# Two-layer transformer trunk: MLP in two phases through DRAM, with seven block products for the latents' first product

## The chip, the cores and the metric

The kernel runs on one core of one Trainium2 chip. The metric is the device time of one execution in microseconds (us); lower is better. A core has TensorE (PE, matrix products), VectorE (DVE), ScalarE (ACT), GpSimd (POOL) and SyncE (SP), which here only issues DMAs. Each engine works through its own instructions in the order in which they stand; semaphores make one wait for another. PE reads its operands from SBUF and writes to PSUM banks, from which DVE and ACT read.

## The reference, cut to what matters

Two layers over 1024 latent tokens and 256 context tokens with 1024 features. Layer 0 mixes tokens by latent attention, layer 1 by neighbourhood attention; each is followed by a squared-ReLU MLP. Layer 1 needs the MLP of the latents alone.

```
def _mlp(h, w1, w2):
    return jnp.square(jax.nn.relu(h @ w1)) @ w2          # w1 1024 x 4096, w2 4096 x 1024

for i in range(2):
    ...
    x = _layer_norm(alpha * x + g1 * y, ln1_g[i], ln1_b[i])        # y: mixer
    x = _layer_norm(alpha * x + g2 * _mlp(x * (1 + sc2) + sh2, mlp_w1[i], mlp_w2[i]), ln2_g[i], ln2_b[i])
    # the context tokens likewise, in layer 0 only
```

## The kernel before, in words

**Arithmetic.** Every large product is made in f32 accuracy from three matmuls in a reduced format: an operand is cut into hi (a cast) and lo (the rest), and `mm3` (L63 to L67) issues hi·hi, hi·lo and lo·hi into one PSUM bank. `split_sb` (L57) makes hi by an ACT cast (L59) and lo by a subtraction on POOL or DVE (L61).

**Tokens and chunks.** Group 0 is the context (256 tokens, tiles 0 and 1), groups 1 and 2 are the latents (512 tokens each, tiles 2 to 5 and 6 to 9). The 4096 hidden features are 32 chunks of 128 (NFF), the 1024 inputs 8 slices k of 128 (KD).

**wo()** multiplies the attention's output by w_o, a token tile at a time, adds the residual, normalises (`normalise`: bn_stats on DVE, a power on POOL at L230, the last step on ACT at L549) and calls `to_hT` for each pair of tiles: PE transposes (L562), ACT applies the modulation (L566), and DVE and POOL split the result into hi and lo (`hTm`). So the MLP's input is split pair by pair.

**mlp()** goes through steps of two chunks for one group. In a step, for each chunk, the first product `pu` takes 8 slices × 3 matmuls (512 columns for a latent group, 256 for the context); ACT and DVE square the ReLU (L817, L818), ACT casts hi (`uh`) and POOL makes lo (`ul`). The second product of the step before stands behind it on PE: for each token tile two halves `py` of 2 chunks × 3 matmuls of 512 columns, added into `y` in SBUF by DVE (L778). u stays in SBUF. The last steps of each group also multiply by the gate and add the residual (`prep`, L731 and L732), normalise, and in layer 0 make the next layer's transposes (`hTa`).

**What sets the order.** The program is written in program order, and a scheduler puts each engine's instructions in an order of its own by simulated times. Tiles of a pool are reused: a new one waits until the readers of the old one are done. Weights come through three raw buffers (tag "raw", bufs=3) on SP's DMA queue, in order; stores go on ACT's queue, in order with ACT's other work.

## Time and profile before

| what | value |
|---|---|
| device time, median of 3 runs | 3207.97 us (3207.79 to 3212.2) |
| span of the profiled execution | 3209.5 us |
| PE busy | 3093.2 us, 96% of the span |
| DVE, ACT, POOL busy | 52%, 34%, 34% |
| granted TensorE clock, mean | 0.987 |
| mlp of layer 0 (first pu to last py) | about 872 to 1786 us |
| mlp of layer 1 | about 2466 to 3192.5 us |

The profiled execution is a run like the others: its span of 3209.5 us stands 1.5 us above their median. In a window row the busy time of each engine is followed by its number of instructions; what PE's busy time lacks to the window's length is PE's idle time. The granted clock is a share of 2.4 GHz; 0.5 is 1.2 GHz.

### The profile page before, as it was taken

What the parts mean: (1) busy time and instruction counts of PE and PEld (TensorE: products, weight loads), DVE (VectorE), ACT (ScalarE), POOL (GpSimd) and SP (SyncE); (2) the same over time, 40 slices, a digit from 0 to 9 for tenths busy, and PEclk for the clock granted to TensorE, in tenths of its full rate; (3) what the DMA queues carried; (4) which work ended last, traced back from release to release, by engine and by line L of the source; (5) the groups of instructions that cost most, each with busy time, mean ns of one, the idle gap of its engine ahead of it and who ended that gap; (6) DMA issues with size and microseconds to landing.
All of it is one profiled execution on the core that took longest, in us unless ns stands there. A gap on an engine that the chain in (4) does not pass through costs nothing.

```text
span 3209.5 us, 41711 instructions
## 1 busy us (share of the span) xinstructions
PE 3093.2 (96%) x16242; PEld 2590.1 (81%) x16242; DVE 1662.1 (52%) x3590; ACT 1089.9 (34%) x1899; POOL 1083.8 (34%) x772
## 2 busy tenths in 40 slices
PE   8999999999999999999998899999988999999996
PEld 4798888798878888888887788888867888888885
DVE  4345666575623333333348777777758333333358
ACT  2234444443432121111124455555543412212222
POOL 3352111112224343433227422233224344443236
PEclk8999999999999999999999999999999999999998
DMA  8445332304412111112113211111144222221122
GB/s 322 156 165 177 127 122 96 124 24 139 157 59 67 52 60 59 53 60 68 38 60 112 78 45 48 44 45 41 39 133 156 66 74 71 73 86 53 53 72 99
DMA packets 106646, 286.57 MB, mean 89 GB/s; under 512 B 9984, under 2 KB 43904, under 8 KB 100688
## 3 DMA queue, kind: packets, MB, share of 16 engines
q1 hardware_dynamic: 79536, 229.84, 21.8%
q10 hardware_dynamic: 26912, 54.05, 4.5%
q8 instruction: 128, 2.10, 0.3%
q14 instruction: 70, 0.57, 0.1%
HBM read 231.40 MB, written 52.46 MB: 88 GB/s over the span
## 4 chain that ended last, share of the span: by engine, by line
PE 85%; DVE 8%; ACT 2%; DMA 2%; issue 1%; POOL 1%; SPq 0%; ACTq 0%; DVEq 0%; POOLq 0%
PE py L65 9%; PE py L66 9%; PE py L67 9%; PE pu L65 8%; PE pu L66 8%; PE pu L67 8%; PE nj L66 3%; PE nj L65 3%; PE nj L67 3%; PE pt L487 2%; PE mps L151 2%; PE s L464 1%; PE po L66 1%; PE s L465 1%; PE s L467 1%
## 5 line engine op out<-in xcount | busy, mean ns | idle before, releaser
L778 DVE TENSOR_TENSOR y<-py,y 128x512 f32<-128x512 f32 x496 | 341.7, 691 | 533.4 <-PE py L67 533.2
L65 PE MATMUL py<-w2h,uh 128*128 128x512 f32 x1152 | 449.3, 393 | 22.3 <-DVE y L758 12.8
L66 PE MATMUL py<-w2l,uh 128*128 128x512 f32 x1152 | 448.5, 391 | 0.0
L67 PE MATMUL py<-w2h,ul 128*128 128x512 f32 x1152 | 447.3, 390 | 0.0
L61 POOL TENSOR_TENSOR ul<-r,uh 128x512 fp32r<-128x512 f32 (+1 forms) x160 | 195.0, 1219 | 419.3 <-ACT uh L59 396.6
L65 PE MATMUL pu<-hTm,whw 128*128 128x512 f32 (+1 forms) x880 | 325.9, 371 | 4.0 <-DVE r L818 3.4
L66 PE MATMUL pu<-hTm,whw 128*128 128x512 f32 (+1 forms) x880 | 325.9, 370 | 0.0
L67 PE MATMUL pu<-hTm,wlw 128*128 128x512 f32 (+1 forms) x880 | 325.5, 370 | 0.0
L818 DVE SCALAR_TENSOR_TENSOR r<-pu,r 128x512 f32<-128x512 f32 (+1 forms) x160 | 101.7, 636 | 358.7 <-ACT r L817 357.7
L65 PEld LDWEIGHTS py<-w2h,uh 128*128 128x128 f32 x1152 | 217.6, 189 | 68.2 <-DVE y L758 14.1
L67 PEld LDWEIGHTS py<-w2h,ul 128*128 128x128 f32 x1152 | 216.9, 188 | 45.9
L66 PEld LDWEIGHTS py<-w2l,uh 128*128 128x128 f32 x1152 | 217.2, 189 | 41.7
L817 ACT ACTIVATE r<-pu 128x512 f32<-128x512 f32 (+1 forms) x160 | 88.3, 552 | 447.2 <-PE pu L67 445.0
L476 POOL TENSOR_TENSOR p<-p,st 128x1280 f32<-128x1280 f32 (+1 forms) x40 | 79.2, 1979 | 381.6 <-DVE st L475 298.4
L65 PE MATMUL nj<-hTa,whn 128*128 128x512 f32 (+1 forms) x512 | 200.2, 391 | 2.2 <-ACT njt L864 2.2
L65 PEld LDWEIGHTS pu<-hTm,whw 128*128 128x128 f32 x880 | 166.9, 190 | 33.7 <-DVE r L818 3.7
L66 PEld LDWEIGHTS pu<-hTm,whw 128*128 128x128 f32 x880 | 167.0, 190 | 29.1
L67 PEld LDWEIGHTS pu<-hTm,wlw 128*128 128x128 f32 x880 | 166.9, 190 | 28.4
L67 PE MATMUL nj<-hTa,wln 128*128 128x512 f32 (+1 forms) x512 | 188.4, 368 | 0.0
L66 PE MATMUL nj<-hTa,whn 128*128 128x512 f32 (+1 forms) x512 | 187.6, 366 | 0.0
L61 POOL TENSOR_TENSOR w2l<-w2r,w2h 128x1024 fp32r<-128x1024 f32 x46 | 109.9, 2399 | 172.0 <-PE pu L67 169.6
L54 ACT CAST th<-pt 128x512 fp32r<-128x512 f32 x168 | 96.8, 585 | 162.5 <-PE pt L487 160.7
(270 smaller groups left out, 7262.6 us busy)
## 6 DMA issues: line engine op xcount, KB each, us to landing
adaw<-in_ada_w SPq DMA_DIRECT2D x40, 1024.0 KB
w2r<-in_mlp_w SPq DMA_DIRECT2D x72, 512.0 KB
raww<-in_w SPq DMA_DIRECT2D x50, 512.0 KB
rawn<-in_nqkv SPq DMA_DIRECT2D x24, 512.0 KB
w1rw<-in_w SPq DMA_DIRECT2D x22, 512.0 KB
x1d<-xr ACTq DMA_DIRECT2D x18, 512.0 KB
xa<-x1d SPq DMA_DIRECT2D x18, 512.0 KB
x1e<-xa ACTq DMA_DIRECT2D x18, 512.0 KB
```

Source lines behind the costliest of these rows:

```text
L54: nc.scalar.copy(hi, ps)
L61: return h, e.tensor_tensor(lo, src, self.f(hi), op=ALU.subtract)
L65: mm(out, lhsT=ah, rhs=bh, start=first, stop=False)
L66: mm(out, lhsT=ah, rhs=bl, start=False, stop=False)
L67: return mm(out, lhsT=al, rhs=bh, start=False, stop=last)
L151: nc.tensor.matmul(ps[32 * j:32 * j + 32, :], lhsT=self.sT[:, k, :], rhs=x, start=(k == 0), stop=(k == KD - 1), tile_position=(0, 32 * j))
L464: mm(o, lhsT=qq[:, 0, sl], rhs=kh, start=True, stop=False)
L476: (nc.vector.tensor_scalar(p[:, 0:n], p[:, 0:n], st[:, 5:6], None, op0=ALU.mult) if t % 2 else nc.gpsimd.tensor_tensor(p[:, 0:n], p[:, 0:n ...
L487: nc.tensor.transpose(pt[:, c, i, :], ps_[i][:, col:col + P], self.ident)
L778: nc.vector.tensor_tensor(y[t][:, ns], py, y[t][:, ns], op=ALU.add)
L817: nc.scalar.activation(r[:, 0:n], pu[:, 0:n], AF.Relu)
L818: nc.vector.scalar_tensor_tensor(r[:, 0:n], pu[:, 0:n], 0.0, r[:, 0:n], op0=ALU.max, op1=ALU.mult)
```

## The change

`mlp()` becomes `up()` (the first product, for all chunks) and then `down()` (the second). Between them u goes to DRAM (`ud`) as hi and lo and comes back.

In `up()`, the latents' product is taken as one of 2 × 2 blocks: the inputs' two halves of four slices k, two chunks (f0, f1 of the pair fp), and the two latent groups. Eight block products of 12 matmuls (4 slices × 3) become seven, by the Strassen-Winograd scheme. On the token side it needs A11, A12, A22 and the sums S1 to S4, each cast to hi and lo (once per layer, `split` and `comb`); on the weights' side B11, B21, B12 (with the context), B22 and T1 to T4, made for every pair of chunks (`prepare`). Products that share a summand accumulate in one PSUM bank and are read in between (`p1`, `u2`, `u3`). The context's product in layer 0 keeps its form. `wo()` no longer splits: `to_hF` leaves the modulated transposes in f32 (`hf`), and `up()` splits them.

In `down()`, blocks of 2 or 4 chunks go through all token tiles; u is loaded for each pair of tiles (`ub`, three buffers).

```diff
-    def mlp(self, l, nm, nm2):                     # two-chunk steps, u in SBUF
-            for si, (chunks, g) in enumerate(steps):
...
+    def to_hF(self, xhs, pair, hs, nm):            # called by wo() in place of to_hT
...
+                nc.scalar.activation(self.hf[g][:, k, off:off + 256], pt[:, c, :], AF.Identity,
+                                     scale=hs[:, 0, k:k + 1], bias=hs[:, 1, k:k + 1])
+    def mlp(self, l, nm, nm2, front, hpools=None):
+        self.ud = [[self.dp.tile([P, 2, n], F32, name=f"ud{l}_{f}_{g}") for g, (o, n) in enumerate(GR)]
+                   for f in range(NFF)]
+        self.up(l, nm, front)
+        self.down(l, nm, nm2, hpools)
+    def up(self, l, nm, front):
...
+            def split(n):
+                for j in range(0, 4, 2):
+                    self.split_sb(A[n][0][:, j:j + 2], A[n][1][:, j:j + 2], blk[n][:, j:j + 2], lo_eng="dve")
+            def comb(o, x, y, op):
+                for j in range(0, 4, 2):
+                    nc.vector.tensor_tensor(blk[o][:, j:j + 2], blk[x][:, j:j + 2], blk[y][:, j:j + 2], op=op)
+            split("A11")
+            split("A12")
+            if l == 0:
+                for j in range(0, 8, 4):
+                    self.split_sb(hc[0][:, j:j + 4], hc[1][:, j:j + 4], self.hf[0][:, j:j + 4], lo_eng="dve")
+            split("A22")
+            comb("S1", "A21", "A22", ALU.add)
+            comb("S3", "A11", "A21", ALU.subtract)
+            comb("S2", "S1", "A11", ALU.subtract)
+            split("S2")
+            split("S1")
+            split("S3")
+            comb("S4", "A12", "S2", ALU.subtract)
+            split("S4")
...
+                def X():
+                    h, lo = pair(self.wp, ("wh", "wl"), "x")
+                    self.split_sb(h, lo, raw[0])
+                def Ta():
+                    nc.vector.tensor_tensor(t[:, 0:4], b12, b11, op=ALU.subtract)
+                    nc.vector.tensor_tensor(t[:, 4:8], b22, t[:, 0:4], op=ALU.subtract)
+                    h, lo = pair(self.ws, ("th", "tl"), "a")
+                    self.split_sb(h, lo, t)
...
+            def put(src, f, g, n, nm_):
+                nc.scalar.copy(uhl[:, 0, 0:n], src)
+                nc.vector.tensor_tensor(uhl[:, 1, 0:n], src, self.f(uhl[:, 0, 0:n]), op=ALU.subtract)
+                nc.scalar.dma_start(self.ud[f][g], self.f(uhl[:, :, 0:n]))
+            def from_sb(ps, x, f, g, nm_):
+                nc.vector.tensor_tensor(c, ps, x, op=ALU.add)
+                nc.scalar.activation(c, c, AF.Relu)
+                nc.scalar.activation(c, c, AF.Square)
+                put(c, f, g, 512, nm_)
...
+                prod(pa, B["11"], A["A11"], True, False)
+                p1 = sb("p1")
+                nc.scalar.copy(p1, pa)
+                if fp == 0:
+                    prod(pa, B["21"], A["A12"], False, True)
+                    from_ps(pa, f0, 1, 512, f"a{l}{fp}")
+                    ctx(0, "11", "21")
+                prod(pb, B["T2"], A["S2"], True, False)
+                nc.vector.tensor_tensor(u2, pb, p1, op=ALU.add)
+                prod(pc, B["T1"], A["S1"], True, False)
+                prod(pb, B["T3"], A["S3"], False, False)
+                nc.vector.tensor_tensor(u3, pb, p1, op=ALU.add)
+                from_sb(pc, u3, f1, 2, f"d{l}{fp}")
+                if fp:
+                    prod(pa, B["21"], A["A12"], False, True)
+                    from_ps(pa, f0, 1, 512, f"a{l}{fp}")
+                    ctx(0, "11", "21")
+                prod(pb, B["T4"], A["A22"], False, True)
+                from_sb(pb, p1, f0, 2, f"c{l}{fp}")
+                prod(pc, B["22"], A["S4"], False, True)
+                from_sb(pc, u2, f1, 1, f"b{l}{fp}")
+                ctx(1, "12", "22")
+    def down(self, l, nm, nm2, hpools):
+        sizes = [2, 4, 4, 4, 4, 4, 4, 2, 4]
...
+                    wr = self.wp.tile([P, D], F32, tag="raw", bufs=3, name=f"w2r{l}{f}")
+                    nc.sync.dma_start(wr, a["mlp_w2"][l, f * P:(f + 1) * P, :])
+                    self.split_sb(h, lo, wr)
+            def load(bi, fs, p):
+                u = up.tile([P, 4, 2, 256], F32R, tag="ub", bufs=3, name=f"ub{l}{bi}{p}")
+                for i, f in enumerate(fs):
+                    nc.sync.dma_start(self.f(u[:, i]), self.ud[f][g][:, :, off:off + 256])
```

**Where instructions move, 1.** DVE at the end of wo() and the start of the MLP in layer 0. `mv0a9` is the LayerNorm of the last token tile, `hTm` the split of the last pair, `r` the first chunks' squared ReLU. Before, from the last tile on:

```order
L547 SCALAR_TENSOR_TENSOR mv0a9_9265<-mv0a9_9265 128x1
L59 CAST hTm0200_9059<-htmpm040_9278 128x256
L61 TENSOR_TENSOR hTm0201_9060<-htmpm040_9278,hTm0200_9059 128x256
L59 CAST hTm0210_9061<-htmpm041_9282 128x256
L59 CAST hTm0220_9063<-htmpm042_9291 128x256
```

In the changed kernel the same stretch of DVE holds the lo parts of `A11`, `A12`, `hc` (context) and `A22` (L61), the sums (L704, made in place in `hfm`) and the lo parts of S1 to S4:

```order
L548 SCALAR_TENSOR_TENSOR mv0a9_9124<-mv0a9_9124 128x1
L61 TENSOR_TENSOR A11l0_9263<-hfm01_8608,A11h0_9262 128x1024 x2
L61 TENSOR_TENSOR A12l0_9271<-hfm01_8608,A12h0_9270 128x1024 x2
L61 TENSOR_TENSOR hcl_9277<-hfm00_8431,hch_9276 128x1024 x2
L61 TENSOR_TENSOR A22l0_9273<-hfm02_8957,A22h0_9272 128x1024 x2
L704 TENSOR_TENSOR hfm02_8957<-hfm02_8957 128x1024 x2
L704 TENSOR_TENSOR hfm02_8957<-hfm01_8608,hfm02_8957 128x1024
L61 TENSOR_TENSOR S1l0_9267<-hfm02_8957,S1h0_9266 128x1024
L704 TENSOR_TENSOR hfm02_8957<-hfm01_8608,hfm02_8957 128x1024
L61 TENSOR_TENSOR S1l0_9267<-hfm02_8957,S1h0_9266 128x1024
L704 TENSOR_TENSOR hfm01_8608<-hfm02_8957,hfm01_8608 128x1024
L61 TENSOR_TENSOR S3l0_9269<-hfm02_8957,S3h0_9268 128x1024
```

The splits of the last pair (`hTm`, 128x256) are gone. Eight more rows of the same kind and size follow (24 operations of 128x1024 in all; 22 in layer 1, which has no `hc`), and then the first sums on the weights' side, `ta` and `tb` (128x512), from which ACT and POOL make T1 to T4. On ACT the cast of A11's hi part stands behind the eight `hf` activations of the last pair.

**Where instructions move, 2.** SP between up() and down() of layer 0, in the changed kernel. `w2r` are raw rows of w2, `ub00` the u of the first block for the three first pairs of tiles:

```order
L867 DMA w2r04_12820<-in_mlp_w2 128x1024
L867 DMA w2r05_12826<-in_mlp_w2 128x1024
L867 DMA w2r06_13033<-in_mlp_w2 128x1024
L919 DMA ub000_12773<-ud0_0_0_9163 128x512
L919 DMA ub000_12773<-ud0_1_0_9166 128x512
L919 DMA ub001_12832<-ud0_0_1_9164 128x2x256
L919 DMA ub001_12832<-ud0_1_1_9167 128x2x256
L919 DMA ub002_12867<-ud0_0_1_9164 128x2x256
L919 DMA ub002_12867<-ud0_1_1_9167 128x2x256
L867 DMA w2r07_13039<-in_mlp_w2 128x1024
```

Before, u needed no load, and SP's rows at the start of the MLP were those of the weights, the residual and the gate:

```order
L116 DMA raww1000_9353<-in_w1 128x1024
L116 DMA raww1001_9391<-in_w1 128x1024
L692 DMA w2r000_9429<-in_mlp_w2 128x1024
L692 DMA w2r001_9435<-in_mlp_w2 128x1024
L618 DMA xr08_9127<-in_xtok 128x1024
L618 DMA xr09_9200<-in_xtok 128x1024
L704 DMA w1rw1032_9665<-in_w1 128x1024
L116 DMA raww1033_9703<-in_w1 128x1024
L534 DMA ln1_g0_10041<-in_ln1_g 128x1024
```

The first loads of u stand behind the raw rows of chunks 4, 5 and 6, each of which takes over a raw buffer from chunk 1, 2 or 3. On POOL the lo parts of w2's chunks 0 to 3 stand one behind the other; ACT's cast of chunk 1 takes the buffer that the last product of up() read. Layer 1 has the same order.

**Where instructions move, 3.** ACT within up() of layer 1, around the copy of `p1` for one pair of chunks (`th`, `wh`: weights' hi parts; `cc`, `cb`: two of the four results; `ud`: a store):

```order
L59 CAST th16b_23852<-tb16_23849 128x1024
L786 ACTIVATE cc15_23841<-cc15_23841 128x512
L787 ACTIVATE cc15_23841<-cc15_23841 128x512
L773 CAST uhlc15_23845<-cc15_23841 128x512
L59 CAST wh16y_23876<-w1r113_23732 128x512
L786 ACTIVATE cb15_23868<-cb15_23868 128x512
L775 DMA ud1_10_2_22830<-uhlc15_23845 128x1024
L787 ACTIVATE cb15_23868<-cb15_23868 128x512
L813 COPY p116_23899<-sa16_23884 128x512
L773 CAST uhlb15_23872<-cb15_23868 128x512
```

The copy `p116` of the pair's first block product stands behind the work on the pair before, a store among it, which waits for DVE's lo part. On PE the product that goes on in the same bank (B21·A12) is issued three matmuls behind the end of the first product (of S1's, in another bank); in layer 0 the distance is larger, and ACT has also the context's results and one more cast (`wh`, 128x1024) ahead of the copy.

## Rows read from the trace of the kernel before

**Rows 1.** Page, parts 1 and 4: busy time by engine; the chain by engine.

```profile
PE 3093.2 (96%) x16242; PEld 2590.1 (81%) x16242; DVE 1662.1 (52%) x3590; ACT 1089.9 (34%) x1899; POOL 1083.8 (34%) x772
...
PE 85%; DVE 8%; ACT 2%; DMA 2%; issue 1%; POOL 1%; SPq 0%; ACTq 0%; DVEq 0%; POOLq 0%
```

**Rows 2.** PE in layer 0's MLP: start us, us, line, operation.

```profile
1209.80 0.39 PE L65 MATMUL pu<-hTm,whw 128*128 128x512 f32 x1
...
1212.52 0.39 PE L66 MATMUL py<-w2l,uh 128*128 128x512 f32 x1
```

**Rows 3.** Windows: length, busy us (x instructions) by engine, clock, DMA share, GB/s.

```profile
885.00:890.00 5.00, 1.32 (x8) 0.84 (x8) 4.39 (x13) 3.56 (x8) 2.39 (x4) 0.80 0.41 116
890.00:895.00 5.00, 4.88 (x12) 3.88 (x13) 3.91 (x6) 3.10 (x5) 2.38 (x3) 0.52 0.74 247
...
1690.00:1810.00 120.00, 104.08 (x478) 83.59 (x476) 105.02 (x168) 51.88 (x78) 78.40 (x64) 0.96 0.31 109
2466.00:2490.00 24.00, 17.59 (x76) 13.82 (x75) 21.77 (x47) 11.92 (x17) 10.16 (x11) 0.86 0.58 203
2550.00:2600.00 50.00, 50.00 (x222) 41.41 (x221) 15.79 (x23) 8.67 (x12) 24.11 (x13) 1.00 0.22 73
3120.00:3150.00 30.00, 27.89 (x122) 22.44 (x120) 25.57 (x17) 5.98 (x9) 23.50 (x10) 1.00 0.50 159
3150.00:3160.00 10.00, 0.34 (x1) 0.35 (x2) 8.88 (x8) 1.73 (x3) 5.28 (x3) 0.55 0.27 94
3160.00:3192.00 32.00, 30.67 (x125) 24.80 (x125) 30.42 (x58) 9.36 (x8) 18.97 (x17) 0.93 0.17 67
```

**Rows 4.** Timeline at the end of wo(), layer 0, of DVE, ACT and POOL.

```profile
872.93 1.23 DVE L649 SCALAR_TENSOR_TENSOR xr<-xr,ty 128x1024 f32<-128x1024 f32 x1
874.07 1.22 DVE L61 TENSOR_TENSOR w1lw<-w1rw,w1hw 128x1024 fp32r<-128x1024 f32 x1
875.21 1.28 DVE L543 BATCH_NORM_STATS2 bn0a<-xr 128x6 f32<-128x512 f32 x2
...
877.84 1.24 ACT L549 ACTIVATE xr<-xr,mv0a 128x1024 f32<-128x1024 f32 x1 [7.79 <-DVE mv0a L547]
...
883.95 2.01 ACT L566 ACTIVATE htmpm<-htm,hs 128x256 f32<-128x256 f32 x4 [4.87 <-PE htm L562]
```

**Rows 5.** Groups by line and shape: xcount | busy us, mean ns | idle before.

```profile
L778 DVE TENSOR_TENSOR y<-py,y 128x512 f32<-128x512 f32 x496 | 341.7, 691 | 533.4 <-PE py L67 533.2
...
L61 DVE TENSOR_TENSOR ol<-or,oh 128x1024 fp32r<-128x1024 f32 x18 | 22.2, 1235 | 12.9 <-ACT oh L59 12.9
...
L817 ACT ACTIVATE r<-pu 128x512 f32<-128x512 f32 x128 | 76.1, 594 | 294.7 <-PE pu L67 292.6 <-POOL y L762 0.4
L59 ACT CAST w2h<-w2r 128x1024 fp32r<-128x1024 f32 x72 | 73.8, 1048 | 187.6 <-PE py L67 181.6 <-POOL w2r L694 5.9
...
L61 POOL TENSOR_TENSOR w2l<-w2r,w2h 128x1024 fp32r<-128x1024 f32 x46 | 109.9, 2399 | 172.0 <-PE pu L67 169.6 <-ACT w2h L59 2.4
```

**Rows 6.** POOL and DVE side by side, end of layer 1's MLP.

```profile
3119.80 3.37 POOL L731 TENSOR_TENSOR y<-y,g 128x1024 f32<-128x1024 f32 x1
...
3120.84 3.41 DVE L61 TENSOR_TENSOR wlw<-raww,whw 128x1024 fp32r<-128x1024 f32 x1
...
3125.31 1.87 DVE L778 TENSOR_TENSOR y<-py,y 128x512 f32<-128x512 f32 x3
3128.50 3.40 DVE L732 TENSOR_TENSOR y<-y,xq 128x1024 f32<-128x1024 f32 x1 [1.32 <-POOL y L731]
```

**Rows 7.** A load's issue on SP and the ACT cast that waits for it.

```profile
2426.27 6.36 SPq L116 DMA_DIRECT2D raww<-in_w  x2
...
2429.96 1.05 ACT L59 CAST whw<-raww 128x1024 fp32r<-128x1024 f32 x1 [2.37 <-DMA raww<-in_w]
```

**Rows 8.** Page, part 2: mean data rate in 40 slices of the span.

```profile
GB/s 322 156 165 177 127 122 96 124 24 139 157 59 67 52 60 59 53 60 68 38 60 112 78 45 48 44 45 41 39 133 156 66 74 71 73 86 53 53 72 99
```

More of the change, by code (lines that the diff above doesn't have):

```diff
@@ L568, in to_hT @@
                 self.split_sb(h[:, off:off + 256], lo[:, off:off + 256], tmp, hi_eng="dve", lo_eng="pool" if k % 2 else "dve")
+    def to_hF(self, xhs, pair, hs, nm):
+        nc = self.nc
+        g, off = grp_of(pair * 2)
+        if g not in self.hf:
+            self.hf[g] = self.hfp.tile([P, KD, GR[g][1]], F32, name=f"hf{nm}{g}")
+        for k2 in range(KD // 2):
+            pt = self.bank("t", f"ht{nm}{pair}{k2}", (P, 2, 256))
+            for c in range(2):
+                for i in range(2):
+                    k = k2 * 2 + c
+                    nc.tensor.transpose(pt[:, c, i * P:(i + 1) * P], xhs[i][:, k * P:(k + 1) * P], self.ident)
+            for c in range(2):
+                k = k2 * 2 + c
+                nc.scalar.activation(self.hf[g][:, k, off:off + 256], pt[:, c, :], AF.Identity,
+                                     scale=hs[:, 0, k:k + 1], bias=hs[:, 1, k:k + 1])
     def hT_tiles(self, g, pair, nm):
@@ L678, in mlp, with pool @@
+        pairs = list(range(5)) if l == 0 else list(range(1, 5))
+        with ExitStack() as es:
+            def pool(n, st=es, **kw):
+                return st.enter_context(tc.tile_pool(name=f"{n}{l}", bufs=1, reuse_waits="tile", **kw))
+            up, yp, ep = pool("du"), pool("dy"), pool("de")
+            top = ExitStack()
+            rp, xp = pool("dr", top), pool("dx", top)
+            y = {t: yp.tile([P, D], F32, name=f"y{l}{t}") for p in pairs for t in (2 * p, 2 * p + 1)}
             gates, aff = {}, []
-            tail = [True]
@@ L831, in mlp, with products @@
-            down(*pend)
+            def load(bi, fs, p):
+                g, off = grp_of(2 * p)
+                u = up.tile([P, 4, 2, 256], F32R, tag="ub", bufs=3, name=f"ub{l}{bi}{p}")
+                for i, f in enumerate(fs):
+                    nc.sync.dma_start(self.f(u[:, i]), self.ud[f][g][:, :, off:off + 256])
+                return u
+            def products(bi, t, i, u, w2, n):
+                ns = slice(n * 512, (n + 1) * 512)
+                sl = slice(i * P, (i + 1) * P)
+                py = self.bank("ud"[n], f"py{l}{bi}{t}{n}")
+                for c, (wh, wl) in enumerate(w2):
+                    self.mm3(py, u[:, c, 0, sl], u[:, c, 1, sl], wh[:, ns], wl[:, ns], c == 0, c == len(w2) - 1)
+                return py, ns
@@ new lines, in down, with half @@
+            order = sorted(y)
+            f = 0
+            blocks = []
+            for n in sizes:
+                blocks.append(list(range(f, f + n)))
+                f += n
+            w2 = weights(0, blocks[0])
+            for bi, fs in enumerate(blocks):
+                final = bi == len(blocks) - 1
+                if final:
+                    top.close()
+                    if hpools:
+                        hpools()
+                nw = None
+                for p in pairs:
+                    v = 1 if p == 0 else 0
+                    u = load(bi, fs, p)
+                    for i in range(2):
+                        t = 2 * p + i
+                        if final:
+                            pys = [products(bi, t, i, u, w2, n) for n in range(2)]
+                            def half(n, t=t, pys=pys):
+                                py, ns = pys[n]
+                                if l == 1:
+                                    nc.vector.tensor_tensor(y[t][:, ns], py, y[t][:, ns], op=ALU.add)
+                                    return
+                                ty = ep.tile([P, 512], F32, tag="r", bufs=2, name=f"ty{l}{t}{n}")
+                                nc.vector.tensor_tensor(ty, py, gates[v][:, ns], op=ALU.mult)
+                                nc.gpsimd.tensor_tensor(y[t][:, ns], y[t][:, ns], ty, op=ALU.add)
+                            self.normalise(ep, f"{l}m{t}", y[t], y[t], half, 2 if l == 1 and t == 9 else 1)
+                            if l == 1:
+                                emit(t)
+                                continue
+                            if t >= 2:
+                                self.x2[t] = self.dp.tile([P, D], F32, name=f"x2d{t}")
+                                nc.scalar.dma_start(self.x2[t], y[t])
+                            if i == 1:
+                                self.to_hT(ep, ("htmp", 256), [y[t - 1], y[t]], p, self.hs[1][v], nm2)
+                            continue
+                        for n in range(2):
+                            py, ns = products(bi, t, i, u, w2, n)
+                            if bi == 0:
+                                nc.scalar.copy(y[t][:, ns], py)
+                            else:
+                                nc.vector.tensor_tensor(y[t][:, ns], py, y[t][:, ns], op=ALU.add)
+                        if bi == len(blocks) - 2:
+                            prep(t, v)
+                    if nw is None and not final:
+                        nw = weights(bi + 1, blocks[bi + 1])
+                    if 1 <= bi < len(blocks) - 2 and order:
+                        residual(order.pop(0))
+                w2 = nw
@@ L1077, in run @@
         self.attn1("a1", last)
[L1078 removed]
+        st, f = front(1)
         self.wo(1, a["w_o1"], lambda t: self.x2[t], 2, "m1", box)
         w.close()
[L1081 removed]
+        self.mlp(1, "m1", None, f)
+        st.close()
 def layout(i):
```

243 lines of the change are left out of this document (112 added, 131 removed).

## Prediction, on record before the result was known

> **What bounds the kernel now.** I read the page first: PE is busy 96% of the span and carries 85% of the chain that ended last, DVE 8% [rows 1]. So a matmul taken away is worth its interval, as long as PE is not left waiting in its place. That interval comes from the timeline of PE in the MLP: twelve matmuls of 512 columns lie between the starts 1209.80 and 1212.52, 0.2267 us each; the 0.39 shown is the modelled duration, not the spacing [rows 2]. The window 2550 to 2600 agrees, with 222 matmuls in 50 us and no idle time [rows 3]. Then I looked for the places where PE does wait around the MLPs. Between wo() and the MLP of layer 0 it is idle for 3.7 us in 885 to 890, and right after that the granted clock is 0.52, about 1.2 GHz: 12 matmuls in 5 us instead of 22, so a restart costs about 2.3 us more [rows 3]. With a little idle time just before, layer 0 loses about 7 us there. In layer 1 it is 6.4 us idle in 2466 to 2490 and, at clock 0.86 over 17.6 busy us, 2.5 more: 9. At the end of layer 0's MLP, 1690 to 1810, 15.9 us are idle and the clock of 0.96 takes 4: 20, with DVE busy 105 of 120 us. At the end of layer 1's, 3120 to 3192, idle time is 2.1 + 9.7 + 1.3 and the clock takes 2: 15 [rows 3].
>
> **What it removes.** Each of 16 pairs of chunks has 7 × 12 matmuls for the latents in place of 8 × 12, in two layers: 16 × 12 × 2 = 384 matmuls × 0.2267 = 87.1 us. All of it is on PE. The additions into y are halved too (blocks of four chunks instead of two), but DVE's 691 ns each [rows 5] lie beside 12 matmuls (2.72 us) already, so that gives nothing. What it does give is at the two ends: in the last block every tile now has 24 matmuls, 5.44 us, beside DVE's roughly 5 us of gate, statistics and splits (an estimate from its 128x512 and 128x1024 durations), where the 12 of before left PE waiting. Of layer 0's 20 us I let 6 stay (a LayerNorm, below, still ends the layer): gain 14. Layer 1's 15 us go, since the gate and residual are now put in a block earlier: gain 15. Sum of the gains: 116.
>
> **What it adds between wo() and up().** This is the largest cost. The trace shows what follows the last matmul of wo(), at about 872.2: DVE's multiplication and sum, statistics, a power on POOL, and the ACT step that ends at 879.1 [rows 4]. Without the weight split of 1.14 in between, that is 6 us behind the last matmul. Then the eight modulations of the last pair on ACT, four of which took 2.01 [rows 4]: hf is done at about 10.6. Only then ACT casts A11 (1.05 [rows 5]), at 11.7, and DVE starts on its 24 operations of 128x1024. Such operations start 1.14 apart where they follow each other (872.93, 874.07, 875.21 [rows 4]) and last 1.23 [rows 4, 5]: 27.4 to 29.5 us, done at 39.1 by the first. Three operations of 128x512 for ta and tb, about 2.0; the cast of T1 and T2 1.05; POOL's lo part 2.40 [rows 5]: 44.6 us after wo()'s last matmul. In that time PE has the last transposes (about 1.2), two block products (24 × 0.2267 = 5.4), the context's 24 matmuls of half the width (2.7) and a few matmuls with T's hi part (0.9): 10.2. So 34.4 are lost, 36.7 with a restart at the low clock, against 7 before: +29.7. Layer 1 has 22 operations and no context: 42.3 less 7.5, plus 2.3, against 9: +28.1. Together 58; with 1.23 for each operation 62.
>
> **Between up() and down().** The first u cannot be loaded before SP has issued three raw rows of w2 that wait for POOL's lo parts of chunks 1, 2 and 3, and the cast of chunk 1 waits for the last product of up(). So from that product's end: cast 1.05, three POOL operations of 2.40 [rows 5], then issue and landing. A load issued at 2426.27 let its cast start at 2429.96, 3.7 us later [rows 7]. Sum 12.0 us of idle PE and 2.3 of restart, in both layers: 28.5. Before, PE went on without a break.
>
> **Within up().** In layer 1 p1 must be copied out before B21·A12 goes on in the same bank. The copy is like L817, 594 ns [rows 5], and starts behind a matmul that lasts 0.39; PE has three matmuls (0.68) to cover it: about 0.3 us lost for each of 15 pairs, 5. It also stands behind ACT's work on the pair before, which just fits; I take 8. Bounds: 0, and 36 when each copy is late by one POOL operation of 2.40. In layer 0 the copy is wanted later, but behind a store that waits for DVE's lo part, a weight cast and the context's results. DVE operations with both operands in SBUF got longer beside POOL: one began at 3120.84 beside a POOL operation of 3119.80 to 3123.17 and took 3.41 in place of 1.23, and another 3.40 at 3128.50; the additions with a PSUM operand beside them kept 0.62 each [rows 6]. By that a copy in layer 0 comes 0 to 1.9 us late (2.40 less half a us of slack): 0 to 28 over 15 pairs. I take 13, nearly the middle, because the additions in the chain read PSUM and only the lo parts and the weights' sums meet POOL. The first pairs, whose preparations begin only when the long chain is through, 4. In down() the gating of y on POOL (2.40 to 3.37 each) and weights' lo parts meet DVE's additions in the last blocks but one: 4.5 in both layers. Elsewhere down() is 12 or 24 matmuls a half or whole tile against one addition, and PE-bound.
>
> The Trainium skill (SBUF — State Buffer, "Who interferes with whom") says that a DVE instruction with two SBUF inputs and a GpSimd instruction that reads SBUF block each other for the whole instruction, and that one with at most one SBUF input doesn't. The trace agrees in both halves [rows 6]. It speaks against this change, which moves the lo parts of u from POOL to DVE and adds sums of weights there, while POOL goes on splitting weights. Were each meeting to fall on the copy of p1, the sum would be that of the slower rival below.
>
> **The sum.** Costs 58 + 28.5 + 8 + 13 + 4 + 4.5 = 116, against 116 gained. The profiled execution of 3209.5 would stay 3209.5; it stands 1.5 above the median of the runs, which gives 3208. I take 3207, because the attention's last stage before wo() has fewer splits beside it, worth a us at most.
>
> **Rivals.** *Faster:* the stalls within up() are hidden and only the boundaries cost. For it speaks that in layer 1's window PE had no idle time with DVE at 32% and POOL at 48% [rows 3], so meetings are few; against it, the thin cover of p1. Both terms gone: 3207 − 21 = 3186.
>
> *Slower:* the in-order queue of ACT. A store waits for a lo part on DVE, that for a POOL operation, and p1's copy stands behind the store. It decides from the point where the copy ends later than PE's other work in the pair, 0.7 us behind the product in layer 1. At the upper bounds, 36 + 28 in place of 21: +43, 3250. For it: 8.4 us of POOL's weights splits in each 19 us of layer 1 (three of 2.40 and a half). Against: DVE's two-SBUF operations, about eight of 0.69, fill under a third of a pair, so not every copy is met.
>
> *The removed matmuls were not on the path,* or the way through DRAM is too slow. Layer 0's down() reads 42 MB of u and 17 of weights in 1920 × 0.2267 = 435 us: 136 GB/s, where the first slice of the span shows 322 [rows 8]. If no matmul's time came back, 3207 + 87 = 3294. PE's 96% speaks against it.
>
> **Chances.** Forecast 0.55, faster rival 0.22, slower 0.18, the last 0.05. A difference under 0.2% (6.4 us) can't be told from none. The forecast's own range is 3190 to 3228: down by both stalls at their low ends, up by layer 0's stall at its bound and the chain at 1.23. Of its 0.55, 0.19 lie faster by over 0.2%, 0.22 within and 0.14 slower. With the rivals: faster 0.41, same 0.22, slower 0.37. The range for 8 in 10 reaches towards both rivals: 3178 to 3244.
>
> **What would show it.** In the changed profile: PE idle for about 34 us behind wo() in both layers, with DVE's 128x1024 operations back to back there; about 12 us idle between up() and down(); in up() of layer 1 a matmul rate near 84 in 19.0 us, with gaps of a few tenths released by ACT's p1; the idle times at both MLPs' ends down to a few us. It would be wrong if A11's cast ran before the last hf, if the first u were loaded without a wait for w2, or if gaps of over 1 us stood in every pair.

## The result, and the profile of the changed kernel

The changed kernel takes 3235.97 us (median of four runs, 3235.61 to 3236.79), the kernel before 3208.99 (four runs): a ratio of 1.0082, interval 1.0068 to 1.0097. It is slower by 27 us, where the forecast was no change (3207, range 3178 to 3244). The profiled execution spans 3233.9 us against 3209.5, so its trace has 24.4 of the 27 to show.

The page, parts 1 and 4, answers to [rows 1].

```profile
PE 3035.4 (94%) x15858; PEld 2524.3 (78%) x15858; DVE 1755.8 (54%) x3584; ACT 1231.0 (38%) x2105; POOL 1103.3 (34%) x680
...
PE 75%; DVE 10%; issue 6%; ACT 4%; DMA 3%; POOL 2%; SPq 0%; ACTq 0%; DVEq 0%; POOLq 0%
```

The 384 matmuls are gone (16242 to 15858), and PE's busy time fell by 58 us, not by 87: some matmuls got slower (below), and more of them run at the low clock (mean granted clock 0.973 over the span, 0.987 before). What grew is PE's idle time, the span less the busy time: from 116.3 to 198.5 us (its share of the chain went from 85% to 75%). The costliest waits of PE, with their total, how often and the longest:

```profile
PE sa L66 <- ACT p L813: 40.6, 8, 20.5
PE py L66 <- DMA ub<-ud: 37.5, 2, 19.1
PE py L66 <- ACT oh L59: 14.5, 2, 12.9
```

The first two are the boundaries that the prediction priced, ahead of up() and of down(). The third lies in wo(), whose products the diff doesn't touch. Windows of the changed kernel, in the columns of [rows 3]:

```profile
745.00:775.00 30.00, 16.39 (x84) 13.53 (x82) 11.93 (x12) 11.29 (x14) 7.20 (x3) 0.77 0.60 203
...
884.00:930.00 46.00, 18.65 (x67) 14.40 (x65) 34.27 (x37) 24.21 (x29) 4.03 (x3) 0.63 0.10 34
...
1145.00:1245.00 100.00, 99.48 (x527) 85.76 (x526) 60.50 (x72) 48.76 (x80) 39.12 (x16) 1.00 0.41 146
1320.00:1345.00 25.00, 5.89 (x32) 5.12 (x31) 11.85 (x7) 8.52 (x12) 20.63 (x9) 0.63 0.98 348
...
1710.00:1830.00 120.00, 109.93 (x511) 88.66 (x510) 100.20 (x163) 38.90 (x60) 91.12 (x69) 0.97 0.44 149
2545.00:2840.00 295.00, 292.54 (x1271) 237.02 (x1270) 151.13 (x210) 159.72 (x243) 136.76 (x60) 1.00 0.45 163
...
3170.00:3215.00 45.00, 45.00 (x200) 37.20 (x199) 41.09 (x62) 6.22 (x5) 33.58 (x20) 1.00 0.48 166
```

745 to 775 is the beginning of wo() in layer 0, where PE stands still for 13.6 of 30 us. Before, the same stretch was full:

```profile
745.00:775.00 30.00, 29.49 (x172) 25.64 (x172) 11.71 (x15) 9.97 (x15) 6.17 (x3) 1.00 0.45 137
```

Within up(), 1145 to 1245 in layer 0 and 2545 to 2840 in layer 1, PE is idle for 0.5 and 2.5 us, far from the 21 that had been priced for stalls (what is left of them stands under "Within up()" below). At 1320 to 1345, between up() and down(), it is idle for 19.1. The end of layer 0's MLP, 1710 to 1830, keeps 10 idle us; that of layer 1's has none.

**The wait in wo().** ACT in the changed kernel, start, length, line, operation and, in brackets, its idle time and what ended it:

```profile
753.48 2.94 ACT L59 CAST woh<-wor 128x1024 fp32r<-128x1024 f32 x3 [2.49 <-DVE o L496]
764.41 1.04 ACT L59 CAST oh<-or 128x1024 fp32r<-128x1024 f32 x1 [7.99 <-DMA or<-od]
```

The same two in the kernel before:

```profile
732.45 2.95 ACT L59 CAST woh<-wor 128x1024 fp32r<-128x1024 f32 x3
...
740.13 1.05 ACT L59 CAST oh<-or 128x1024 fp32r<-128x1024 f32 x1 [3.16 <-DMA or<-od]
```

The cast of wo's first weights went back by 21 us, behind the attention's last casts, and oh by 24; wo()'s last matmul went from about 872 to 883.7. The change opens the pools ws and hf ahead of wo(), so wo's tiles got other memory, which comes free only when the attention is done: in the built layout `woh` lies in the memory of the attention's k and q tiles, where before it lay in that of the modulation's weights, which were done with early.

**Ahead of up(), layer 0**, to be read against [rows 4]. The long chain in the timeline:

```profile
883.74 0.39 PE L68 MATMUL py<-woh,ol 128*128 128x512 f32 x1
...
890.16 1.54 PE L582 MATMUL htm<-ident,xr 128*128 128x128 f32 x6 [5.80 <-ACT xr L550]
...
896.24 0.79 PE L66 MATMUL sa<-A11h,wh00x 128*128 128x512 f32 x1 [2.05 <-ACT A11h L59]
...
896.22 2.36 DVE L61 TENSOR_TENSOR A11l<-hfm,A11h 128x1024 fp32r<-128x1024 f32 x2 [7.39 <-ACT A11h L59]
898.50 2.35 DVE L61 TENSOR_TENSOR A12l<-hfm,A12h 128x1024 fp32r<-128x1024 f32 x2
...
921.21 2.35 DVE L61 TENSOR_TENSOR S4l<-hfm,S4h 128x1024 fp32r<-128x1024 f32 x2
923.64 0.59 ACT L813 COPY p<-sa 128x512 f32<-128x512 f32 x1 [2.42 <-DVE S4l L61]
924.28 0.80 PE L66 MATMUL sa<-A12h,wh00x 128*128 128x512 f32 x1 [18.56 <-ACT p L813]
...
929.57 0.63 PE L66 MATMUL sb<-S2h,th00a 128*128 128x512 f32 x1
```

DVE's 24 operations run back to back from 896.22 to 923.5, 1.14 each. PE waits 18.6 us in one piece, for p1's copy: p1's tile lies in the memory of hf (by the built layout), which the last operation of the chain still reads. So B21·A12, taken for work beside the chain, came behind it.

**Ahead of down(), layer 0:**

```profile
1326.66 5.61 POOL L61 TENSOR_TENSOR w2xl<-w2r,w2xh 128x1024 fp32r<-128x1024 f32 x2
...
1332.21 1.65 SPq L867 DMA_DIRECT2D w2r<-in_mlp_w  x3
1334.38 8.78 SPq L919 DMA_DIRECT2D ub<-ud  x6
...
1342.31 0.77 PE L66 MATMUL py<-w2wh,ub 128*128 128x512 f32 x1 [19.11 <-DMA ub<-ud]
```

The chain over POOL is the one foretold; it is through 9.1 us behind the last product (predicted 8.3). But u lands 8 us after its issue and not 3.7 as in [rows 7]: three raw rows of w2 (1.5 MB) stand ahead of it, issued 2.2 us before, and the engines of the DMA are busy throughout (share 0.98).

**Within up(), layer 1.** PE's first matmul of two successive pairs, and between them the last matmul of a pair's first product, p1's copy, and the matmul that goes on in the same bank:

```profile
2621.91 0.39 PE L66 MATMUL sa<-A11h,wh15x 128*128 128x512 f32 x1
...
2634.60 0.39 PE L68 MATMUL sa<-A11h,wl15x 128*128 128x512 f32 x1
...
2635.03 0.59 ACT L813 COPY p<-sa 128x512 f32<-128x512 f32 x1
...
2635.67 0.50 PE L66 MATMUL sa<-A12h,wh15x 128*128 128x512 f32 x1
...
2641.24 0.39 PE L66 MATMUL sa<-A11h,wh16x 128*128 128x512 f32 x1
```

A pair takes 19.33 us, where 84 matmuls × 0.2267 are 19.04.

**A slower matmul.** In down()'s odd blocks, whose weights are the tiles w2x, matmuls start 0.2333 us apart, and in the even blocks 0.2267 as in [rows 2]. The trace shows it as a longer one (duration in ns, lowest/median/highest):

```profile
L66 PE MATMUL py<-w2xh,ub x504: 394/394/394, 1371.8 to 3171.1; 128*128 128x512 f32 x168
...
L66 PE MATMUL py<-w2wh,ub x360: 387/389/767, 1342.3 to 3213.3; 128*128 128x512 f32 x180
```

1512 such matmuls × 0.0066 = 10 us. The tiles w2x start at 160 modulo 256 bytes in the memory of a partition, all other operands of the MLPs' matmuls at 224 (start addresses, here and below, are those of the built kernels' layout).

### The profile page after: what moved, and what is told of

The parts are those of the page before. It is cut to its first block, busy times and chain, and to the rows that moved or that the text cites. A ratio compares the mean times of both kernels' runs of the same rounds, so it can differ in the third digit from the quotient of the medians.

```text
span 3233.9 us, 42098 instructions
## 1 busy us (share of the span) xinstructions
PE 3035.4 (94%) x15858; PEld 2524.3 (78%) x15858; DVE 1755.8 (54%) x3584; ACT 1231.0 (38%) x2105; POOL 1103.3 (34%) x680
## 4 chain that ended last, share of the span: by engine, by line
PE 75%; DVE 10%; issue 6%; ACT 4%; DMA 3%; POOL 2%; SPq 0%; ACTq 0%; DVEq 0%; POOLq 0%
PE py L66 7%; PE py L67 7%; PE py L68 7%; PE nj L66 3%; PE nj L67 3%; PE nj L68 3%; PE sb L66 2%; PE sb L67 2%; PE sb L68 2%; PE pt L488 2%; PE sa L66 2%; PE mps L152 2%; PE sa L67 2%; PE sa L68 2%; PE sc L66 1%
## 5 line engine op out<-in xcount | busy, mean ns | idle before, releaser
L974 DVE TENSOR_TENSOR y<-py,y 128x512 f32<-128x512 f32 x252 | 173.1, 690 | 527.4 <-PE py L68 527.1
L66 PE MATMUL py<-w2xh,ub 128*128 128x512 f32 x504 | 198.6, 394 | 0.0
L67 PE MATMUL py<-w2xl,ub 128*128 128x512 f32 x504 | 198.6, 394 | 0.0
L68 PE MATMUL py<-w2xh,ub 128*128 128x512 f32 x504 | 198.6, 394 | 0.0
L66 PE MATMUL py<-w2wh,ub 128*128 128x512 f32 x360 | 142.9, 397 | 37.5 <-DMA ub<-ud 37.5
L470 DVE TENSOR_SCALAR_CACHE_REDUCE p<-s 128x512 f32<-128x512 f32 (+1 forms) x208 | 117.1, 584 | 57.5 <-PE pt L488 32.6
L55 DVE TENSOR_TENSOR tl<-pt,th 128x512 fp32r<-128x512 f32 x168 | 114.3, 687 | 56.0 <-ACT th L54 55.0
L67 PE MATMUL py<-w2wl,ub 128*128 128x512 f32 x360 | 143.0, 397 | 0.0
L68 PE MATMUL py<-w2wh,ub 128*128 128x512 f32 x360 | 142.3, 395 | 0.0
L59 ACT CAST w2xh<-w2r 128x1024 fp32r<-128x1024 f32 x28 | 28.1, 1044 | 299.1 <-PE py L68 246.1
L1091 ACT ACTIVATE pp<-pp,nst 128x640 f32<-128x640 f32 (+1 forms) x128 | 102.9, 804 | 96.2 <-DVE nst L1089 95.8
L61 POOL TENSOR_TENSOR wln<-rawn,whn 128x1024 fp32r<-128x1024 f32 x28 | 67.4, 2409 | 208.7 <-ACT whn L59 208.6
L66 PE MATMUL py<-woh,oh 128*128 128x512 f32 x288 | 114.2, 400 | 21.6 <-ACT oh L59 14.5
L61 POOL TENSOR_TENSOR w2wl<-w2r,w2wh 128x1024 fp32r<-128x1024 f32 x20 | 47.8, 2412 | 250.1 <-ACT w2wh L59 250.1
L61 POOL TENSOR_TENSOR w2xl<-w2r,w2xh 128x1024 fp32r<-128x1024 f32 x28 | 68.8, 2478 | 186.8 <-ACT w2xh L59 186.8
L67 PE MATMUL py<-wol,oh 128*128 128x512 f32 x288 | 114.8, 400 | 0.0
```

Of the source, the lines that this page charges most:

```text
L55: nc.vector.tensor_tensor(lo, ps, self.f(hi), op=ALU.subtract)
L61: return h, e.tensor_tensor(lo, src, self.f(hi), op=ALU.subtract)
L66: mm(out, lhsT=ah, rhs=bh, start=first, stop=False, skip_group_check=more)
L67: mm(out, lhsT=ah, rhs=bl, start=False, stop=False, skip_group_check=more)
L68: return mm(out, lhsT=al, rhs=bh, start=False, stop=last, skip_group_check=more)
L470: nc.vector.tensor_scalar(p[:, o0:o0 + n], o, 1.0, None, op0=ALU.mult, op1=ALU.max, accum_out=st[:, i:i + 1])
```

## The experiments

Each is an edit of the changed kernel. The theory was that the loss is a sum of four things at the edges (the memory of wo(), the chain ahead of up(), the order of loads ahead of down(), the start of w2x), each curable by itself; the rivals were that a cure moves the wait elsewhere, or that the products themselves don't pay.

**e1_hf_right**: hf on the other side of memory, ws opened only after wo().

```diff
-            ap = pool("ma", side="right")
+            ap = pool("ma", side="right") if l else pool("ma")
...
-            self.ws = pool(st, f"ws{l}")
-            self.hfp, self.hf = pool(f, f"hf{l}"), {}
+            if l:
+                self.ws = pool(st, f"ws{l}")
+            self.hfp, self.hf = pool(f, f"hf{l}", **({} if l else {"side": "right"})), {}
...
         self.wo(0, a["w_o0"], lambda t: a["xtok"][t], 0, "m0")
+        self.ws = pool(st, "ws0")
```

> Only the places of three pools in layer 0 change: hf on the right side, the A tiles on the left, ws opened after wo(); the instructions stay. Theory: hf and ws, opened ahead of wo(), took the memory that was free early, so wo()'s weight tiles had to wait for the end of the attention, and the 12 us by which wo() ended later (883.7 against 872) are that wait. It expects wo()'s last matmul back at 872 and 12 us less, 3224; the order shows that in layer 0 the first loads of u now stand ahead of the raw rows of w2's chunks 4 to 6 as well, which takes up to 8 us more away: 3216 to 3224. Rival: the load of the attention's output (or) lands late because of DMA traffic, whatever the weights' memory: wo() still ends at 884, 3228 to 3236.

3207.74 us (ten runs; ratio to before 0.9993, 0.9983 to 1.0002): 28 less than the changed kernel, more than either theory expected. The stretch in wo() is full again:

```profile
745.00:775.00 30.00, 29.47 (x165) 25.37 (x164) 13.18 (x16) 11.76 (x16) 7.38 (x3) 0.98 0.42 133
```

Ten of the 28 are wo()'s (htm's matmuls behind it start at 880.3, not 890.2). The new layout also freed the first loads of u in layer 0 from the queue of w2: PE waits 4.1 and 2.2 us there in place of 19.1. The wait for p1 is 16.1 in place of 18.6. In layer 1, where the layout is as it was, it still waits 18.3. So the edit isn't a pure test of wo(), but what it says is plain: where pools lie, and the order of loads that comes of it, was worth all that the kernel had lost.

**e2_u_first**: the first three pairs' loads of u are issued ahead of the second block's weights.

```diff
+                us = {}
+                if bi == 0:
+                    us = {p: load(bi, fs, p) for p in pairs[:3]}
+                    nw = self.after(lambda: weights(1, blocks[1]), ld[0])
                 for p in pairs:
-                    u = load(bi, fs, p)
+                    u = us.pop(p) if p in us else load(bi, fs, p)
```

> Both layers: the loads of u for the first three pairs of tiles are issued ahead of w2's chunks 2 to 6. Theory: the 19.1 and 18.4 us of idle PE between up() and down() are 9 us of waiting behind three POOL operations plus 8 us of landing behind 1.5 MB of w2. It expects the idle time down to the cast of chunk 1 and one POOL operation, about 4 us, in each layer: 2 x 15 less, 3206. Rival: the wait is for the w2 weights (chunk 1's split, which needs the last product's buffer) or for the stores of u, so that only the landing gets shorter: 2 x 7 less, 3222.

3220.95 us (1.0036, 1.0021 to 1.0050), 15 less: half of what the theory said, and near the rival's 3222. Loads on SP and the matmul that waits, layer 0:

```profile
1326.15 9.53 SPq L921 DMA_DIRECT2D ub<-ud  x6
...
1335.78 8.19 SPq L867 DMA_DIRECT2D w2r<-in_mlp_w  x3
...
1330.62 0.77 PE L66 MATMUL py<-w2wh,ub 128*128 128x512 f32 x1 [5.87 <-DMA ub<-ud]
```

With u in front the wait is 5.9 us in layer 0 (19.1 before the edit). In layer 1 it is still 10.6: there u stands on SP behind a row of the next LayerNorm whose memory comes free late, a wait that had been hidden under the first. So the figure is the rival's, but the mechanism isn't: 13 and 8 us of these waits are gone, not 7 and 7, and new waits of 2.1 us (for the u of a later pair of tiles, layer 0) and 2.2 us (for ACT's copy of y, layer 1) take a part back.

**e3_chain_short**: the first pair's ta, tb and p1 get memory of their own and are prepared ahead of the chain, and S1, S3 and S4 come after S2's split.

```diff
-            split("S2")
-            split("S1")
-            split("S3")
-            comb("S4", "A12", "S2", ALU.subtract)
-            split("S4")
+            self.after(rest, split("S2"))   # rest(): S1, S3, S4 as above
...
-                p1 = sb("p1")
+                p1 = sb("p1") if fp else p10
```

> Both layers: T1 to T4 of the first pair of chunks and p1's tile get memory of their own and are made ahead of the chain on DVE, and S2's sums and split come ahead of S1's and S3's. Same arithmetic. Theory: the 36 us and 39 us lost between wo() and up() are DVE's chain of 24 (22) operations plus ta, th and tl behind it; T2 x S2 can start after 16 (14) operations: 10 to 14 us less in each layer, 3208 to 3216. Rival: PE's restart or the first tiles of the results, whose memory is free only when the chain ends, hold it anyway: under 4 us a layer, 3228 to 3236.

3221.93 us (1.0039, 1.0024 to 1.0054), 14 less, between the theory's 20 to 28 and the rival's 8. In the traces the way from wo()'s last matmul to up()'s last became 10 us shorter in layer 0 and 6 in layer 1. The wait of 18.6 us is gone in layer 0, and a new one stands behind it:

```profile
911.16 0.50 PE L66 MATMUL sa<-A11h,wh01x 128*128 128x512 f32 x1 [0.91 <-ACT wh01x L59]
...
920.18 0.79 PE L68 MATMUL sa<-A11h,wl01x 128*128 128x512 f32 x1 [8.07 <-POOL wl01x L61]
```

The second pair's weights are late, since ta had taken a raw weight buffer. That wait is of the edit's own making; e6 lays ta elsewhere. The edit does three things at once (p1's memory, T's sums ahead, S2 first), and how the 14 us divide among them isn't shown.

**e4_pad64**: 64 bytes ahead of w2x, which then starts at 224 modulo 256 like the rest.

```diff
+            ep.tile([P, 16], F32, name=f"pad{l}")
             top = ExitStack()
```

> One tile of 64 bytes per partition is added in down() ahead of the pool with the odd blocks' weights, so that these start 96 bytes behind a multiple of 128, as all other matmul operands do, in place of 32. Theory: the matmuls of the odd blocks start 0.2333 us apart, those of the even blocks 0.2268, because of that start address; it expects 0.2268 in all blocks and 9 to 10 us less, 3226. Rival: the odd blocks are slow for what runs beside them (loads of w2 and u, splits), so 0.2333 stays and the time too, 3236.

3229.0 us (1.0057, 1.0042 to 1.0072), 7 less, where 9 to 10 were expected; in the traces down() is 5 and 6 us shorter in the two layers. The interval in odd blocks is 0.2267, and the duration that of all others:

```profile
L66 PE MATMUL py<-w2xh,ub x504: 389/389/389, 1373.3 to 3163.1; 128*128 128x512 f32 x168
```

**e5_eight_products**: the changed kernel's two phases, with the eight products of before in place of Strassen's seven (the sums S and T left out).

```diff
-            for n in ("A11", "S2", "S1", "S3", "A12", "A22", "S4"):
+            for n in ("A11", "A12", "A21", "A22"):
...
+                        prod(ps, B["11" if c == 0 else "12"], A["A11" if g == 1 else "A21"], True, False)
+                        prod(ps, B["21" if c == 0 else "22"], A["A12" if g == 1 else "A22"], False, True)
```

> The changed kernel with eight block products instead of seven: A11, A12, A21 and A22 alone are split, no sums S and T, no p1, u2, u3; everything else, with the way through DRAM and the places of the pools, stays. Theory: the 384 matmuls less are worth their 87 us, and the chain that makes S costs about 20 us a layer more than plain splits (10 operations of 128x1024 in layer 0, 8 in layer 1, and the products can follow them one by one): 3236 + 87 - 40 = 3283 (3272 to 3290). Rival: the seven products' chain, waits and extra work on DVE, ACT and POOL eat what they save: 3236 or less.

3257.83 us (1.0152, 1.0137 to 1.0167): 22 more than with seven products, where 47 was expected. The short preparation costs PE only about 13 us of idle time ahead of up() in layer 0, in place of 27, and 12.0 ahead of down(), in place of 19, so the seven products give back more of their 87 than I had thought. Even so they pay; it is the two phases as laid out that cost.

**e6_all_four**: e1 to e4 together, with ta no longer in a weight buffer and the rows of the next LayerNorm issued behind the first u.

```diff
-                    gates[v] = self.bcast(ep, self.grow[l][1][v], f"g2{l}{v}", f"row{v}")
+                    gates[v] = bc(ep, self.grow[l][1][v], f"g2{l}{v}", f"row{v}")   # bc: bcast() after the first u
...
-                        residual(order.pop(0))
+                        self.after(lambda: residual(order.pop(0)), ld0)
```

> The four edits together (pools of layer 0, u's first loads ahead, short chain, 64 bytes of padding), with two of them taken further: in layer 1 also the loads of the residual and of the gate and LayerNorm rows stand behind u's first loads, and T1 to T4 of the first pair are made in one tile of their own instead of the raw weight buffers. Theory: they are separate stages of PE's path. From 3236: 28 + 15 + 14 + 7 less, 13 of them counted twice in layer 0, and 8 + 5 more for the two that go further: 3236 - 64 = 3172 (3164 to 3182), below the 3209 of the kernel before. Rival: a wait moves on to the next stage, as idle time ahead of the seven products of the second pair of chunks: 3185 to 3200.

3182.06 us (3180.57 to 3183.52; 0.9916, 0.9901 to 0.9931): 27 below the kernel before and 54 below the changed one, and so the fastest of all. It is 10 above the 3172 of the sum, at the upper end of its range, and the rival's wait, ahead of the second pair's weights, is there with 2.6 us. What PE still waits for around the two edges of layer 0 (the last row stands 21 us into down()):

```profile
900.96 0.79 PE L68 MATMUL sa<-A11h,wl01x 128*128 128x512 f32 x1 [2.58 <-POOL wl01x L61]
...
920.94 0.79 PE L66 MATMUL sb<-S3h,th00b 128*128 128x512 f32 x1 [4.87 <-DVE u L827]
...
1325.92 0.76 PE L66 MATMUL py<-w2wh,ub 128*128 128x512 f32 x1 [3.05 <-DMA ub<-ud]
```

**e7_all_four_eight**: e5 with the edits of e1, e4 and the loads of e6.

> Eight products as in the run of that name, with the pools of layer 0, u's first loads and the padding as in the run with all four edits (there is no chain of sums to shorten). Theory: 87 us more matmuls than the run with all four, less some 10 us a layer for the shorter chain: 3172 + 87 - 20 = 3239 (3228 to 3250), so that the way through DRAM alone, without the seven products, does not beat the kernel before. Rival: what the two phases save at the ends is more than that, 3209 or less.

3211.76 us (ten runs; 1.0009, 0.9999 to 1.0019), the same as before. The forecast of 3239 missed by 27; the rival's 3209 was nearer. So the two phases alone, well laid, change nothing that these runs can tell, and Strassen's seven products are worth 30 us net of their 87.

**e8_shift32, e9_all_at_0, e10_all_at_0_mod_256**: what makes a matmul 0.2333. Pads move the operands' starts: 32 bytes at the low end of memory (all three), 96 or 224 at the high end (e9; e10), 64 ahead of w2x as in e4 (e9, e10).

```diff
+        cp.tile([P, 8], F32, name="pad")
...
+        es.enter_context(tc.tile_pool(name="padr", bufs=1, side="right")).tile([P, 56], F32, name="padr")
```

> The changed kernel with 32 bytes of padding at the start of SBUF: everything allocated from the left starts 32 bytes later (w, th, u and the even blocks' w2 at a multiple of 128, the odd blocks' w2 64 behind one); the A tiles on the right stay at 96. Same instructions. Theory: the interval of matmuls goes with the start address of the moving operand alone: it stays 0.2267 in up() (A at 96), and shows in down() what 0 and 64 give; if a multiple of 64 is best, both kinds of blocks are at or under 0.2267, 10 us or more less than 3236. Rival: the odd blocks' interval belongs to those tiles' place among the others (another bank), not to the address within 128 bytes: 0.2333 stays, 3236.

> Relative to the changed kernel: a 32-byte pad at the start of memory (as in e8_shift32), one of 96 bytes at the other end, and the 64 bytes of e4_pad64 before the odd blocks' weights, so that both operands of every matmul of the MLPs start at 0 mod 128 bytes, where those of the kernel before start at 96. Theory (the interval of two matmuls is 0.2267 us when both operands start alike modulo 128 bytes, whatever the start itself, and 0.2333 when they differ): 0.2267 everywhere, odd blocks of down() and up() too, and a time as of e4_pad64, 3226 to 3232 us. Rival (operands at 96 are what is good, and the pad on the left is bad in itself): 0.2333 in up() at least, as in e8_shift32, and 3245 to 3260 us.

> e9_all_at_0 refuted the rule modulo 128: both operands of up()'s matmuls started at 0 mod 128 there, and the interval stayed 0.233. Taken modulo 256 its up() had the weights at 0 and the A blocks at 128, its down() both at 0 (0.2267). Here the same pads at the left, and 224 bytes at the other end in place of 96, laid from the end of the first attention on: both operands of every matmul of the MLPs start at 0 mod 256 bytes. New theory (0.2267 when both operands start alike modulo 256 bytes, 0.2333 when not): 0.2267 in up() and down() alike, and a time as of e4_pad64, 3226 to 3232 us. Rival (the left pad slows up() in another way, or a start of 224 is what up() wants): 0.233 in up() again and 3246 to 3256 us.

e8 took 3258.84 us (1.0157, 1.0142 to 1.0172), e9 3252.1 (1.0131, 1.0114 to 1.0148), e10 3226.58 (1.0050, 1.0032 to 1.0068). The spacing of the 512-column matmuls in layer 0, worked out from the starts in the timeline, beside both operands' starts modulo 256 (moving / stationary):

| kernel | up() | down(), even blocks | down(), odd blocks |
|---|---|---|---|
| changed | 224/224: 0.228 | 224/224: 0.2270 | 160/224: 0.2333 |
| e4 | 224/224: 0.228 | 224/224: 0.2269 | 224/224: 0.2267 |
| e8 | 224/0: 0.2333 | 0/0: 0.2270 | 192/0: 0.2333 |
| e9 | 128/0: 0.2328 | 0/0: 0.2269 | 0/0: 0.2267 |
| e10 | 0/0: 0.228 | 0/0: 0.2269 | 0/0: 0.2267 |

(The 0.228 has the first pairs in it; in layer 1 it is 0.2271 in the changed kernel and 0.2270 in e10.) e8's time is in neither of its forecasts; it refuted what I held first, that the moving operand's own start decides: its even blocks run at 0.2270 with a start of 0 and its up() at 0.2333 with an untouched 224. e9 refuted the second rule, alike modulo 128. Alike modulo 256 fits all fifteen cells, and e10, made to test it, came out in the range foretold. A larger modulus isn't needed: in e4's odd blocks the starts modulo 512 are 480 and 224, and the interval is 0.2267. Why it is so, these runs don't show.

The 25.5 us between e9 and e10 are not the interval alone: 2688 matmuls × 0.006 = 16. The rest is a wait that the changed kernel had just escaped. One pair of e9, layer 1:

```profile
2638.17 1.30 POOL L61 TENSOR_TENSOR wl15y<-w1r,wh15y 128x512 fp32r<-128x512 f32 x1
2638.24 1.77 DVE L776 TENSOR_TENSOR uhlc<-cc,uhlc 128x512 fp32r<-128x512 f32 x1
...
2640.95 0.57 ACT L815 COPY p<-sa 128x512 f32<-128x512 f32 x1
...
2641.57 0.50 PE L66 MATMUL sa<-A12h,wh15x 128*128 128x512 f32 x1 [0.96 <-ACT p L815]
```

The same pair in the changed kernel:

```profile
2633.37 0.68 DVE L774 TENSOR_TENSOR uhlc<-cc,uhlc 128x512 fp32r<-128x512 f32 x1
2633.37 1.83 POOL L61 TENSOR_TENSOR wl15y<-w1r,wh15y 128x512 fp32r<-128x512 f32 x1
2633.97 1.79 DVE L759 TENSOR_TENSOR tb<-w1r 128x512 f32<-128x512 f32 x1
```

In e9 POOL began 0.07 us ahead of DVE, uhlc took 1.77 us instead of 0.68, its store and p1's copy behind it on ACT went late, and PE waited 0.96. In the changed kernel both begin at once, uhlc keeps its 0.68, and the long one is tb, which ACT takes up 13 us later. So it is in all 14 pairs of layer 1 between the first and the last: uhlc takes 1.77 to 1.78 us in e9, where POOL is 0.07 to 0.08 us ahead each time, and 0.68 to 0.74 in the changed kernel, where POOL begins with it or later. Why POOL comes first in e9 isn't shown. PE's waits for p1 come to 52.2 us in e9 and 40.5 in e10: 12 us, which with 16 makes 28 against the 25.5 measured.

## Why the prediction was wrong, step by step

The working was a sum of large terms that came to nothing. Term by term, in us (cost above zero):

| term | predicted | in the trace |
|---|---|---|
| 384 matmuls | −87 | −87 |
| ends of the two MLPs | −29 | −22 |
| ahead of up(), two layers | +58 | +59 |
| ahead of down(), two layers | +28.5 | +42 |
| p1 within up(), and the first pairs | +25 | +6 |
| last blocks of down() | +4.5 | 0 |
| attention's end and wo() | −1 | +15 |
| interval in odd blocks | not in the sum | +10 |
| tail of the program | not in the sum | +1.4 |
| sum | −1 | +24 |

The profiled spans differ by 24.4, and the terms are good to a us or two. The sum missed 49 us of cost (16 in wo(), 13.5 ahead of down(), 7 at the ends, 10 of interval, 1 ahead of up(), 1.4 in the tail) and had 24 too much (19 within up(), 4.5 in the last blocks).

**What failed first is "the attention's last stage before wo() has fewer splits beside it, worth a us at most".** It looked at instructions alone. The diff moves the opening of two pools ahead of wo(), and with it the memory, and so the time, of wo's tiles: +12 us in layer 0, shown by the rows of ACT, of which e1 takes 10 back. The 3 us more of layer 1's wo() are a difference of the two traces, whose cause no run shows. Nothing in the profile of before shows this; the order of the pools in the diff does.

**Ahead of up()** the time was right (PE's loss of 36.0 us against 7 before in layer 0 is +29.0, predicted 29.7; +29.8 in layer 1, predicted 28.1): from wo()'s last matmul to T2·S2's first are 45.5 us, predicted 44.6. Its parts were not all right, and that they came to the same sum is in part luck. B21·A12 ran behind the chain, beside the split of T2, and not beside the chain: T2's lo part was ready at 928.89, 44.8 us behind wo()'s last matmul, but PE, at the low clock, was through with B21·A12 at 929.57 only. And of the 36.0 us just 27 are idle time (46.00 less 18.65 in the window 884 to 930) where 34.4 were worked out; the other 9 are matmuls at the low clock (0.63 in that window), priced at 2.3. That the chain holds PE is shown by the row of the 18.56 us and by e3, which shortens it and gets a part of the time back.

**Ahead of down()** the mechanism was right and the landing was mis-sized. The 3.7 us of [rows 7] is a load that had the queues to itself; here it waits behind 1.5 MB: 19.1 + 2.2 and 18.4 + 2.2 us in place of 12.0 + 2.3. The restart at the low clock is as priced. e2 puts u first, PE goes on 4.5 us after its issue in layer 0, and the kernel gets 15 us back.

**Within up()** 21 us were taken for stalls, and about 6 came. In layer 1 the base of the term was right: a pair loses 0.29 us (19.33 against 19.04) where 0.3 had been worked out, 4.4 in all, and the 3 us laid on top for ACT's other work did not come. In layer 0, where 13 had been taken, the copy stands 2.7 to 4.6 us behind its product, in ACT's queue, but PE has other products until then and waits 0.26 us in six of the pairs. When they meet, uhlc or tb takes 1.77 to 1.79 us in place of 0.68, and POOL's operation 1.83 in place of 1.30. The Trainium skill (SBUF — State Buffer, "Who interferes with whom") has it that a DVE instruction with two SBUF inputs and a GpSimd instruction that reads SBUF block each other; the trace agrees. Who is hit here goes with which began first, by 0.07 us. So the slower rival's mechanism is real, as e9 shows at 0.96 us a pair, and it was not what made this kernel slower. For layer 0 I had taken nearly the middle of two ends, and the lower came; layer 1, in the changed kernel and in e9, shows that the outcome is a step and not a mean.

**The interval in odd blocks** was in no step: I took 0.2267 for every matmul, from a kernel in which the operands of all matmuls of the MLPs happened to start alike.

**The ends**: layer 1's 15 us were right. Of layer 0's 20 only 7 came, not 14: of the 10 idle us that stay, 3.0 are a wait of the transposes into the next layer (for ACT's y at 1755) and 7 lie behind the last product, at the start of the next layer, and the clock takes 3 more. The contention in the last blocks cost nothing.

The faster rival (only the boundaries cost) was nearly right inside up(), but took over the forecast's price of the boundaries, which was too low; the last rival, that the matmuls were not on the path, is refuted by e5 and e7: with all eight products the kernel is 22 us slower as it was laid out and 30 us with the edges mended.

## What to carry to other kernels

When a change opens or reorders pools, list every tile whose memory moves, those of untouched stages too, and ask when that memory comes free: here it was worth the 27 us that the change lost (e1), 10 of them in wo() and 13 through the order of the loads of u. Price a load at a phase boundary with the bytes queued ahead of it, and put what the next matmul needs first. A stall that hangs on which of two engines begins first came here in every pair or in none; give it a chance, not half its price.
